# The first norm row of a two-layer decoder trunk: its DMA first in the queue, read from PSUM by the first token tile, the second tile's products behind the first's lo parts

## The chip, the core and the metric

The kernel runs on one core of one Trainium2 chip. The metric is device time in microseconds (us) of one execution. Each version is executed several times; a median of the runs is compared, and one execution is taken by the hardware profiler.

## What is computed

The input `x` has 512 tokens of 1024 features, float32. Two layers follow each other; each is

```python
h = rms_norm(x, pre_mix_norm)
proj = h @ w_in
...
mix = jnp.concatenate([y_ssd, y_sb, y_moba], axis=-1) @ w_out
x = x + rms_norm(mix, post_mix_norm)
h2 = rms_norm(x, pre_ffn_norm)
f = (jax.nn.silu(h2 @ w_gate) * (h2 @ w_up)) @ w_down
return x + rms_norm(f, post_ffn_norm)
```

The mixer in the middle has a state-space part, a stick-breaking attention and a block-sparse attention. For this document only the very first line of the first layer matters: `rms_norm(x, w)` scales each token by one over the root of its mean square and each feature by its gain, `w`, a row of 1024 numbers that is the same for all tokens. The projections behind it are matrix products of the normalised tokens with `w_in`.

## The kernel before, in words

Tokens are cut into four tiles of 128 (`NT`), features into eight of 128 (`KT`). Every float32 product is made of three: an operand is split (`split`, lines 115 to 117) into a hi part, a rounded copy that ScalarE (ACT) writes, and a lo part, the rest, that VectorE (DVE) subtracts. `PASSES` (line 142) multiplies hi by hi, hi by lo and lo by hi, all into one PSUM bank.

The weights come from HBM in chunks of 128 x 1024. `chunk` (line 134) takes a raw buffer from a ring of three, issues its DMA on SyncE's queue (SP) and splits it into a hi and a lo buffer from rings of four.

Before the layers the kernel does this. `load_x` (line 105) loads a token tile as two halves of 512 features. The gain row of the first norm has to stand in all 128 partitions. Each half of it is loaded into one partition (line 125), a matrix product with a column of ones spreads it over a PSUM bank (B6 and B7, line 126), and DVE copies it to SBUF (`grow`, line 127). In lines 249 to 255 the first four weight chunks, which are those of the first projection, are asked for, and every token tile goes through `pre_norm` (line 190). ACT squares and sums each half (line 193); a small add on DVE (line 169) and a power on GpSimd (line 170) make the scale of each token; for each half DVE multiplies tile, scale and row in one instruction (line 196); TensorE transposes the result in eight blocks of 128 x 128 (`to_fm`, line 179) into two banks, B[2t] and B[2t+1] for tile t; and `to_hT` splits each bank into the hi and lo tiles `hT` of the normalised, transposed input.

`tok_proj` (line 211) is the first user of these. For each token tile it runs over the eight feature tiles and the three passes, 24 products of 512 columns into one bank (line 219): B0 for tile 0, B2 for tile 1 and so on, so banks that the transposes of the same tile were written to. Two feature tiles use one weight chunk, so a token tile needs four chunks.

The order on every engine is not that of the source. A planner goes through a simulated time line of the whole program and gives each free engine the ready instruction that stands first in priority: the place in the source, moved ahead by an offset where `tc.high_priority` stands. Splits of chunks are moved ahead by 800 (`SPLIT_OFF`), `pre_norm` of tile 0 by 3000 (`NORM_OFF`). `issue_after`, used by `after` (line 145), adds an edge from one instruction to another on the same engine: the second is placed behind the first.

Of the kernel before, what the change touches and what calls it, by code (L numbers as in the profile page):

```python
# [11 lines left out]
AF = mybir.ActivationFunctionType  # L12
OP = mybir.AluOpType
# [3 lines left out]
P = 128  # L17
D = 1024
S = 512
NT = S // P  # L20
# [38 lines left out]
def trunk(ctx, tc, x, wch, wdt, gains, mixgain, conv, small, ident_d, consts_d, stack_d, out):  # L59
    nc = tc.nc  # L60
    V, A, G, T = nc.vector, nc.scalar, nc.gpsimd, nc.tensor
# [5 lines left out]
    def slot(name, dt=F32, n=512):  # L67
        return cp.tile([P, n], dt, name=name, bufs=1)

    def cut(tiles):  # L70
        return [t[:, h * 512:(h + 1) * 512] for t in tiles for h in range(2)]

    F = [None if 4 <= i < 12 or 18 <= i < 20 or 28 <= i < 40 or i >= 43 else cp.tile([P, 512], F32, name=f"F{i}")
         for i in range(NF)]
    DD = [slot(f"D{i}", F32, D) for i in range(6)]
    RR = [slot(f"RR{i}", F32R, D) for i in range(4)]
    hT = [cp.tile([P, KT, 512], F32R, name=f"hT{a}") for a in range(2)]
    B = [ps.tile([P, 512], F32, name=f"B{i}") for i in range(8)]
# [8 lines left out]
    def sm(n):  # L87
        if used[0] + n > 768:
            used[0] = 0
        used[0] += n  # L90
        return SM[:, used[0] - n:used[0]]

    def ring(items):
        n = [0]

        def take():
            n[0] += 1
            return items[(n[0] - 1) % len(items)]
        return take

    xres = [[slot(f"x{t}{h}") for h in range(2)] for t in range(NT)]
    xsave = dr.tile([NT, P, D], F32, name="xsave")
    ident = cp.tile([P, P], F32, name="ident")

    def load_x(t, src):
        for hf in range(2):
            nc.sync.dma_start(xres[t][hf], src[t][:, hf * 512:(hf + 1) * 512])
# [7 lines left out]
    def split(src, hi, lo, eng=V):  # L115
        A.activation(hi, src, AF.Copy)  # L116
        return eng.tensor_tensor(lo, src, hi.bitcast(F32), op=OP.subtract)  # L117

    load_x(0, x)
    nc.sync.dma_start(ident, ident_d)  # L120
    grow, one = F[20:22], F[24][0:1, 0:P]
    V.memset(one, 1.0)
    for hf in range(2):
        row = F[22 + hf][0:1, :]
        nc.sync.dma_start(row, bass.AP(tensor=gains.tensor, offset=gains[0, 0].offset + hf * 512, ap=[[0, 1], [1, 512]]))
        T.matmul(B[6 + hf], one, row, start=True, stop=True)
        V.tensor_copy(grow[hf], B[6 + hf])
    load_x(1, x)
    mhalf = cp.tile([P, 4], F32, name="mhalf")
    V.memset(mhalf, -0.5)  # L130
# [3 lines left out]
    def chunk(l, i, to=None):  # L134
        raw = take_raw()
        hi, lo = to or (take_hi(), take_lo())
        nc.sync.dma_start(raw, wch[l, i])
        with tc.high_priority(offset=SPLIT_OFF):
            split(raw, hi, lo, G if i in POOL_LO else V)
        return hi, lo  # L140
# [4 lines left out]
    def after(instructions):  # L145
        st = ExitStack()
        for i in instructions:
            st.enter_context(tc.issue_after(i.ins))
        return st
# [14 lines left out]
    def rstd_of(ss_ap, n, rest=None):  # L164
        m, r = sm(n), sm(n)
        if rest is None:
            V.tensor_scalar(m, ss_ap, EPS, None, op0=OP.add)
        else:
            V.tensor_scalar(m, ss_ap, rest, EPS, op0=OP.add, op1=OP.add)
        G.tensor_tensor(r, m, mhalf[:, 0:n], op=OP.pow)  # L170
        return r

    def to_fm(srcs, dst, bank):

        for q in range(0, len(srcs), 4):
            n = min(4, len(srcs) - q)
            p = bank()
            for i in range(n):
                T.transpose(p[:, i * P:(i + 1) * P], srcs[q + i], ident)
            dst(q, n, p)  # L180

    def to_hT(t, keep=None):
        def dst(q, n, p):
            sl = slice(t * P, (t + 1) * P)
            split(p.rearrange("p (k l) -> p k l", k=4), hT[0][:, q:q + n, sl], hT[1][:, q:q + n, sl])
            if keep is not None:
                A.activation(keep[q // 4], p, AF.Copy)
        return dst

    def pre_norm(t, grow, jk, bank, keep=None):  # L190
        ssp = sm(2)
        for hf in range(2):
            A.activation(jk[hf], xres[t][hf], AF.Square, scale=1.0 / 32, accum_out=ssp[:, hf:hf + 1])
        r = rstd_of(ssp[:, 0:1], 1, ssp[:, 1:2])
        for hf in range(2):
            V.scalar_tensor_tensor(jk[hf], xres[t][hf], r[:, 0:1], grow[hf], op0=OP.mult, op1=OP.mult)
        to_fm([jk[i // 4][:, (i % 4) * P:(i % 4 + 1) * P] for i in range(KT)], to_hT(t, keep), bank)

    def post_norm(t, banks, grow, jk, sq, store=None):
# [32 lines left out]
    def fm_proj(l, c, p):  # L232
        w = chunk(l, c)
        fm_mm(p, w, 0, NT, True)
        return p
# [9 lines left out]
    take_jk = ring([F[0:2], F[2:4], F[43:45]])  # L245
# [4 lines left out]
    for t in range(NT):  # L250
        first.append(chunk(0, C_V + t))
        if t > 1:
            load_x(t, x)
        with tc.high_priority(offset=0 if t else NORM_OFF):
            pre_norm(t, grow, take_jk(), ring(B[2 * t:2 * t + 2]))

    cst = cp.tile([P, 2 * P + 512 + 2], F32, name="cst")
    triu = cst[:, 0:P]
# [19 lines left out]
    for l in range(DEPTH):  # L278
# [91 lines left out]
        n = 0  # L370
# [60 lines left out]
        r = rstd_of(ss, 4)  # L431
        for j in range(NT):
            V.scalar_tensor_tensor(MIXA[j][:, 0:256], MIXA[j][:, 0:256], r[:, j:j + 1], MG[1][:, 0:256],
                                   op0=OP.mult, op1=OP.mult)
# [6 lines left out]
        for j in range(NT):  # L441
            w = (j + 1) * P
            sume = sm(4)
            for h in range(4):
# [6 lines left out]
                                       op0=OP.add, op1=OP.min, accum_out=nm[:, 0:1])  # L451
# [7 lines left out]
                for i in range(j + 1):  # L459
                    T.matmul(pv[:, h * 64:(h + 1) * 64], pTs[:, i * P:(i + 1) * P],  # L460
                             VT[i][:, 256 + h * 64:256 + (h + 1) * 64], start=h == 0 and i == 0,
                             stop=h == 3 and i == j, skip_group_check=True)
# [7 lines left out]
            r = rstd_of(ss, 1)  # L470
# [10 lines left out]
        for i in range(8):  # L481
            p = fm_proj(l, C_XBC + i, acc())
            u = XBC[i]
            with tc.high_priority(offset=CONV_OFF):
                A.activation(u, p, AF.Identity, bias=cw[:, i, 4:5], scale=cw[:, i, 3:4])
                for j in range(1, 4):
                    V.scalar_tensor_tensor(u[:, j:], p[:, :S - j], cw[:, i, 3 - j:4 - j], u[:, j:],
                                           op0=OP.mult, op1=OP.add)
# [7 lines left out]
        for c in range(NT):  # L496
            with tc.high_priority(offset=SSD_OFF):
                sl = slice(c * P, (c + 1) * P)
# [27 lines left out]
                for g in range(2):  # L526
# [3 lines left out]
                    for h in range(4):  # L530
                        hh = g * 4 + h
                        T.matmul(py[:, hh * 64:(hh + 1) * 64], L[:, h * P:(h + 1) * P], xdt[:, hh * 64:(hh + 1) * 64],  # L532
                                 start=hh == 0, stop=hh == 7, skip_group_check=True)
                V.tensor_tensor(xd, py, xd, op=OP.add)
                if c > 0:
                    po = mx()
                    for g in range(2):
                        T.matmul(po[:, g * 256:(g + 1) * 256], XBC[6 + g][:, sl], state[:, g * 256:(g + 1) * 256],
                                 start=g == 0, stop=g == 1, skip_group_check=True)
# [17 lines left out]
                r = rstd_of(ss, 2)  # L557
                for g in range(2):
                    gs = slice(g * 256, (g + 1) * 256)
                    V.scalar_tensor_tensor(xd[:, gs], xd[:, gs], r[:, g:g + 1], MG[0][:, gs], op0=OP.mult,  # L560
                                           op1=OP.mult)
# [15 lines left out]
        for pair in range(2):  # L577
            toks = (2 * pair, 2 * pair + 1)
            for q, src in ((1, MIXA), (0, MIX)):
                for j in toks:  # L580
                    p = OB[j][q]
                    with tc.high_priority(offset=MIXT_OFF):
                        for i in range(4):
                            T.transpose(p[:, i * P:(i + 1) * P], src[j][:, i * P:(i + 1) * P], ident)
                        split(p, R[(j % 2) * 4 + q], R[(j % 2) * 4 + 2 + q])
            ks = (4, 5, 6, 7, 0, 1, 2, 3) if pair == 0 else (0, 1, 2, 3, 4, 5, 6, 7)
            for k in ks[0:4]:
                w = w_out[k] if pair else chunk(l, C_OUT + k)
                for j in toks:
                    out_mm(j, k, w, ks)  # L590
            for k in ks[4:8]:
                w_out[k] = chunk(l, C_OUT + k)
            for j in toks:
                for k in ks[4:8]:
                    out_mm(j, k, w_out[k], ks)
                with tc.high_priority(offset=NORM_OFF):
                    post_norm(j, OB[j], grow1, take_jk(), MIXA[j])
                    pre_norm(j, grow2, take_jk(), ring(OB[j] if j < 2 else OB[j][0:1]), QA[j])
# [114 lines left out]
        for t in range(NT):  # L713
            for halves in ((0,), (1,)) if t == NT - 1 else ((0, 1),):
                for i, w, gs in tail:
                    down(i, t, w, gs, halves)
            with tc.high_priority(offset=NORM_OFF):
                post_norm(t, B[2 * t:2 * t + 2], grow3, take_jk(), GT[t], store=out if l + 1 == DEPTH else xsave)
                if l + 1 < DEPTH:
                    pre_norm(t, grow4, take_jk(), ring(B[2 * t:2 * t + 2]))  # L720
# [57 lines left out]
```

## Time and profile before

| | us |
|---|---|
| median of 3 runs | 1231.62 (1230.8, 1231.62, 1232.99) |
| the profiled execution | 1231.86 |
| its span, first to last instruction | 1230.0 |
| mean granted TensorE clock of it | 0.998 |
| TensorE (PE) busy | 1209.0 |
| PE's weight loads busy | 1081.8 |
| DVE busy | 872.0 |
| ACT busy | 604.6 |
| GpSimd (POOL) busy | 52.6 |

A busy time is a sum over the whole span; engines work beside each other. All rows come from the one profiled execution, so they add up to its span and not to the median. In a timeline row an instruction or a run of like instructions stands with its start, the time from there to the end of the last, its engine, its line in the kernel, the tile that it writes and those that it reads, its form, and how many it is. What its engine waited for just before stands in brackets. PEld is the weight load of TensorE, and SPq the DMA queue of SyncE.

### The profile page before, as it was taken

The numbers are of one execution on the slowest core, as the hardware profiler recorded it, in microseconds if no ns is written. First come the engines' busy times: TensorE is split into PE (matmuls) and PEld (weight loads), VectorE is DVE, ScalarE is ACT, GpSimd is POOL, SyncE is SP. The second block draws the span as 40 slices with busy tenths as digits, with TensorE's granted clock in tenths as the row PEclk, the third lists the DMA queues.
The fourth block names the chain that finished last, engine by engine and source line by source line (L and its number), as shares of the span: only waits on it lengthen the run. The fifth ranks groups of instructions, "written<-read, shape, count | busy, mean of one in ns | idle before, by whom it ended". The sixth has DMA issues, their size and how long they took to land.

```text
span 1230.0 us, 19124 instructions
## 1 busy us (share of the span) xinstructions
PE 1209.0 (98%) x7562; PEld 1081.8 (88%) x7562; DVE 872.0 (71%) x1526; ACT 604.6 (49%) x1124; POOL 52.6 (4%) x88
## 2 busy tenths in 40 slices
PE   8999999999999999999999999999999999999997
PEld 6887888889999999888887788888999999998886
DVE  5466856889999998434465577478898899983343
ACT  5556764466444444433445666535654444453231
POOL 1010000010000000000010100001000000000000
PEclk9999999999999999999999999999999999999999
DMA  6332233242333332423423322122523333333321
GB/s 230 120 99 86 76 102 103 70 154 87 104 104 103 107 108 96 130 93 120 137 86 104 133 74 80 67 95 70 171 69 104 104 108 108 110 109 116 99 73 69
DMA packets 40494, 128.42 MB, mean 104 GB/s; under 512 B 5426, under 2 KB 5714, under 8 KB 40404
## 3 DMA queue, kind: packets, MB, share of 16 engines
q1 hardware_dynamic: 39060, 122.97, 30.4%
q0 software_dynamic: 1344, 4.23, 1.0%
q8 instruction: 59, 0.97, 0.3%
q14 instruction: 31, 0.25, 0.1%
HBM read 122.95 MB, written 4.23 MB: 103 GB/s over the span
## 4 chain that ended last, share of the span: by engine, by line
PE 88%; DVE 5%; DMA 2%; ACT 2%; issue 1%; DVEq 0%; POOLq 0%; POOL 0%; ACTq 0%
PE B L631 26%; PE B L698 19%; PE B L228 17%; PE B L219 7%; PE B L572 7%; DMA wr<-in_wch_dram 2%; PE B L347 2%; DVE wl L117 2%; PE B L354 1%; PE B L460 1%; ACT wh L116 1%; PE B L325 1%; PE B L532 1%; PE B L326 1%; PE B L456 1%
## 5 line engine op out<-in xcount | busy, mean ns | idle before, releaser
L117 DVE TENSOR_TENSOR wl<-wr,wh 128x1024 fp32r<-128x1024 f32 (+1 forms) x198 | 219.8, 1113 | 79.7 <-ACT wh L116 78.5
L116 ACT ACTIVATE wh<-wr 128x1024 fp32r<-128x1024 f32 (+1 forms) x198 | 191.3, 968 | 132.2 <-PE B L631 66.1
L228 PE MATMUL B<-hT,wh 128*128 128x512 f32 (+1 forms) x768 | 215.3, 361 | 3.6 <-ACT F L314 2.2
L631 PE MATMUL B<-hT,wh 128*128 128x256 f32 x960 | 193.3, 283 | 0.8 <-ACT F L669 0.7
L631 PE MATMUL B<-D,wh 128*128 128x256 f32 x960 | 185.6, 283 | 0.5 <-ACT wh L116 0.4
L698 PE MATMUL B<-wh,RR 128*128 128x512 f32 x608 | 164.8, 389 | 0.0
L631 PEld LDWEIGHTS B<-hT,wh 128*128 128x128 f32 x960 | 158.1, 192 | 1.6 <-ACT F L669 1.3
L228 PEld LDWEIGHTS B<-hT,wh 128*128 128x128 f32 x768 | 136.0, 190 | 23.4 <-ACT F L314 3.3
L631 PEld LDWEIGHTS B<-D,wh 128*128 128x128 f32 x960 | 154.4, 192 | 1.2 <-ACT wh L116 0.6
L116 ACT ACTIVATE wh<-RR 128x512 fp32r<-128x512 f32 (+1 forms) x120 | 89.2, 770 | 109.1 <-PE B L631 46.5
L228 PE MATMUL B<-hT,wl 128*128 128x512 f32 (+1 forms) x384 | 137.8, 360 | 0.0
L631 PE MATMUL B<-hT,wl 128*128 128x256 f32 x480 | 136.1, 283 | 0.6 <-DVE wl L117 0.4
L631 PE MATMUL B<-D,wl 128*128 128x256 f32 x480 | 135.5, 283 | 0.0
L698 PEld LDWEIGHTS B<-wh,RR 128*128 128x128 f32 x608 | 114.0, 188 | 23.5
L117 DVE TENSOR_TENSOR wl<-RR,wh 128x512 fp32r<-128x512 f32 (+1 forms) x120 | 102.2, 864 | 10.8 <-ACT wh L116 8.7
L117 DVE TENSOR_TENSOR RR<-F,RR 128x512 fp32r<-128x512 f32 x48 | 33.1, 691 | 101.3 <-ACT RR L116 101.3
L698 PE MATMUL B<-wl,RR 128*128 128x512 f32 x304 | 95.4, 389 | 0.0
L631 PEld LDWEIGHTS B<-hT,wl 128*128 128x128 f32 x480 | 92.1, 192 | 1.0 <-DVE wl L117 1.0
L631 PEld LDWEIGHTS B<-D,wl 128*128 128x128 f32 x480 | 92.1, 192 | 0.0
L116 ACT ACTIVATE RR<-F 128x512 fp32r<-128x512 f32 x48 | 30.0, 629 | 122.9 <-PE B L698 122.2
L219 PE MATMUL B<-wh,hT 128*128 128x512 f32 x256 | 82.4, 397 | 0.8 <-DVE hT L117 0.8
L228 PEld LDWEIGHTS B<-hT,wl 128*128 128x128 f32 x384 | 73.1, 190 | 8.9
(210 smaller groups left out, 2005.8 us busy)
## 6 DMA issues: line engine op xcount, KB each, us to landing
wr<-in_wch_dram SPq DMA_DIRECT2D x204, 512.0 KB, 3.6
x<-in_x_dram SPq DMA_DIRECT2D x16, 256.0 KB, 2.9
F<-acd POOLq DMA_DIRECT2D x16, 256.0 KB, 6.4
F<-in_gains_dram SPq DMA_DIRECT2D x14, 256.0 KB, 4.4
xsave<-x SPq DMA_DIRECT2D x8, 256.0 KB, 2.3
x<-xsave SPq DMA_DIRECT2D x8, 256.0 KB, 3.3
out_dram<-x SPq DMA_DIRECT2D x8, 256.0 KB, 2.0
D<-in_mixgain_dram SPq DMA_DIRECT2D x4, 256.0 KB, 4.6
```

The source lines that it names most:

```text
L116: A.activation(hi, src, AF.Copy)
L117: return eng.tensor_tensor(lo, src, hi.bitcast(F32), op=OP.subtract)
L219: T.matmul(p, hT[a][:, k, t * P:(t + 1) * P], w[k // 2][b][:, (k % 2) * 512:(k % 2 + 1) * 512], start=n == 0, stop=n == 3 * KT - 1)
L228: T.matmul(p[:, t0 * P:t1 * P], w[b][:, k * P:(k + 1) * P], hT[a][:, k, t0 * P:t1 * P], start=first and n == 0, stop=n == 3 * KT - 1, skip ...
L325: T.matmul(p, tiles[2 + h][:, cs], tiles[h][:, cd], start=True, stop=False, skip_group_check=True)
L326: T.matmul(p, tiles[2 + h][:, cs], tiles[4 + h][:, cd], start=False, stop=stop, skip_group_check=True)
L347: T.matmul(pz[:, o:w], ntri if i2 == i else nones, s2, start=False, stop=i2 == NT - 1 and n == 1, skip_group_check=True)
L354: T.matmul(pv[:, j * 64:(j + 1) * 64], e[:, (j - i) * P:(j - i + 1) * P], VT[i][:, h * 64:(h + 1) * 64], start=i == NT - 1, stop=i == 0 an ...
L456: T.transpose(pT[:, i * P:(i + 1) * P], lg[:, i * P:(i + 1) * P], ident)
L572: T.matmul(OB[j][hf], lt, w[b][:, hf * 512:(hf + 1) * 512], start=k == ks[0] and a == 0 and b == 0, stop=k == ks[-1] and a == 1)
L631: T.matmul(p, w[b][:, half * 512 + k * P:half * 512 + (k + 1) * P], left(j, a, k), start=first and k == 0 and n == 0, stop=k == 3 and n == ...
L698: T.matmul(B[2 * t + hf], gs[a][:, t * P:(t + 1) * P], w[b][:, hf * 512:(hf + 1) * 512], start=i == 0 and a == 0 and b == 0, stop=i == HT ...
```

## The change

Three things are changed. The two DMAs of the gain row, the two products that spread it, and the copies to `grow` stand ahead of the loads of token tile 0 and the identity; the copies are made by ACT instead of DVE. Token tile 0's products with the row (line 196) read the spread row in PSUM (`spread`, B6 and B7) instead of `grow`; the other tiles still read `grow`. And `done[t]` keeps the last lo instruction of a tile's transposed input; the two products of token tile 1 with the row are placed behind `done[0]`, the lo part of tile 0's second half.

```diff
-    load_x(0, x)
-    nc.sync.dma_start(ident, ident_d)
-    grow, one = F[20:22], F[24][0:1, 0:P]
+    grow, spread, one = F[20:22], B[6:8], F[24][0:1, 0:P]
     V.memset(one, 1.0)
     for hf in range(2):
         row = F[22 + hf][0:1, :]
         nc.sync.dma_start(row, bass.AP(tensor=gains.tensor, offset=gains[0, 0].offset + hf * 512, ap=[[0, 1], [1, 512]]))
-        T.matmul(B[6 + hf], one, row, start=True, stop=True)
-        V.tensor_copy(grow[hf], B[6 + hf])
+        T.matmul(spread[hf], one, row, start=True, stop=True)
+        A.activation(grow[hf], spread[hf], AF.Copy)
+    load_x(0, x)
+    nc.sync.dma_start(ident, ident_d)
     load_x(1, x)
...
+    done = [None] * NT
+
     def to_hT(t, keep=None):
         def dst(q, n, p):
             sl = slice(t * P, (t + 1) * P)
-            split(p.rearrange("p (k l) -> p k l", k=4), hT[0][:, q:q + n, sl], hT[1][:, q:q + n, sl])
+            done[t] = split(p.rearrange("p (k l) -> p k l", k=4), hT[0][:, q:q + n, sl], hT[1][:, q:q + n, sl])
...
-    def pre_norm(t, grow, jk, bank, keep=None):
+    def pre_norm(t, grow, jk, bank, keep=None, hold=()):
...
         for hf in range(2):
-            V.scalar_tensor_tensor(jk[hf], xres[t][hf], r[:, 0:1], grow[hf], op0=OP.mult, op1=OP.mult)
+            with after(hold):
+                V.scalar_tensor_tensor(jk[hf], xres[t][hf], r[:, 0:1], grow[hf], op0=OP.mult, op1=OP.mult)
...
-            pre_norm(t, grow, take_jk(), ring(B[2 * t:2 * t + 2]))
+            pre_norm(t, grow if t else spread, take_jk(), ring(B[2 * t:2 * t + 2]), hold=[done[0]] if t == 1 else ())
```

## Rows read from the trace of the kernel before

**Rows 1.** The page, part 1: busy us (share of the span) and instructions of each engine.

```profile
PE 1209.0 (98%) x7562; PEld 1081.8 (88%) x7562; DVE 872.0 (71%) x1526; ACT 604.6 (49%) x1124; POOL 52.6 (4%) x88
```

**Rows 2.** Waits of PE, whole span: us in total, times, longest; largest behind the start.

```profile
PE B L228 <- ACT F L314: 2.2, 4, 0.7
```

**Rows 3.** Timeline of PE, 0 to 24 us.

```profile
4.28 3.75 PE L126 MATMUL B<-F,F 1*128 1x512 f32 x4 [4.28 <-DMA F<-in_gains_dram]
7.96 1.12 PE L179 MATMUL B<-ident,F 128*128 128x128 f32 x4
9.55 2.82 PE L179 MATMUL B<-ident,F 128*128 128x128 f32 x12 [0.48 <-DVE F L196]
12.61 0.79 PE L219 MATMUL B<-wh,hT 128*128 128x512 f32 x1 [0.24 <-DVE hT L117]
13.21 0.63 PE L219 MATMUL B<-wl,hT 128*128 128x512 f32 x1
13.63 0.70 PE L219 MATMUL B<-wh,hT 128*128 128x512 f32 x2
...
```

**Rows 4.** The chain that ended last, in order of time: start us, us, what.

```profile
12.61 9.02 PE B L219 x36
...
23.38 13.62 PE B L219 x60
...
99.97 4.61 PE B L228 x19
...
705.51 6.22 PE B L228 x19
```

**Rows 5.** Timeline of DVE, 0 to 24 us.

```profile
5.27 0.23 DVE L273 CAST identb<-ident 128x128 bf16<-128x128 f32 x1 [4.28 <-DMA ident<-in_ident_dram]
5.41 0.21 DVE L169 TENSOR_SCALAR SM<-SM 128x1 f32<-128x1 f32 x1
6.35 0.69 DVE L127 COPY F<-B 128x512 f32<-128x512 f32 x1 [0.73 <-PE B L126]
7.15 0.75 DVE L196 SCALAR_TENSOR_TENSOR F<-x,SM,F 128x512 f32<-128x512 f32 x1
...
8.06 0.69 DVE L127 COPY F<-B 128x512 f32<-128x512 f32 x1
8.74 2.08 DVE L196 SCALAR_TENSOR_TENSOR F<-x,SM,F 128x512 f32<-128x512 f32 x3
10.74 1.22 DVE L117 TENSOR_TENSOR wl<-wr,wh 128x1024 fp32r<-128x1024 f32 x1
11.88 0.68 DVE L117 TENSOR_TENSOR hT<-B,hT 128x512 fp32r<-128x512 f32 x1
...
20.50 1.22 DVE L117 TENSOR_TENSOR wl<-wr,wh 128x1024 fp32r<-128x1024 f32 x1
```

**Rows 6.** Timeline of SP's DMA queue, 0 to 24 us.

```profile
0.74 0.87 SPq L107 DMA_DIRECT2D x<-in_x_dram  x2
...
2.12 0.61 SPq L125 DMA_DIRECT2D F<-in_gains_dram  x2
```

**Rows 7.** Timeline of ACT, 0 to 24 us.

```profile
3.52 0.63 ACT L193 ACTIVATE F<-x 128x512 f32<-128x512 f32 x1 [1.50 <-DMA x<-in_x_dram]
...
8.47 1.06 ACT L116 ACTIVATE wh<-wr 128x1024 fp32r<-128x1024 f32 x1 [0.64 <-DMA wr<-in_wch_dram]
9.44 0.58 ACT L116 ACTIVATE hT<-B 128x512 fp32r<-128x512 f32 x1
...
19.06 1.06 ACT L116 ACTIVATE wh<-wr 128x1024 fp32r<-128x1024 f32 x1 [1.24 <-DMA wr<-in_wch_dram]
```

**Rows 8.** Timeline of POOL, 0 to 24 us.

```profile
5.77 0.55 POOL L170 TENSOR_TENSOR SM<-SM,mhalf 128x1 f32<-128x1 f32 x1 [2.80 <-DVE SM L169]
```

**Rows 9.** Waits of SP's DMA queue, 0 to 40 us: us in total, times, longest.

```profile
SPq L137 <- DMA cst<-in_consts_dram: 0.7, 1, 0.7
```

**Rows 10.** One stretch: PE, PEld, DVE, ACT, POOL busy, PEclk, DMA share, GB/s.

```profile
708.00:710.00 2.00, 2.00 (x6) 1.52 (x6) 1.08 (x2) 0.27 (x1) 0.00 (x0) 0.50 0.00 0
```

## The prediction

> **What bounds the kernel now.** I read the page first. TensorE (PE) is busy for 1209.0 of 1230.0 us [rows 1], so a change that touches no matmul of the layers can only move what stands before the first of them, or a wait of PE further on. The list of PE's waits says how little there is of the second kind: behind the start the largest group is 2.2 us in four waits [rows 2]. So I read the first 24 us engine by engine. PE's timeline [rows 3] shows the four broadcast matmuls of the norm row at 4.28, the transposes of the first token tile at 7.96, a run of twelve more from 9.55 (four of tile 0, eight of tile 1), and the first projection product at 12.61. From there the chain of waits is PE alone: 36 products to 21.63, then transposes, then 60 products from 23.38 in 13.62 us, 0.227 each [rows 4]. Whatever brings the product of 12.61 forward, and only that, moves the end.
>
> What holds it is VectorE (DVE) [rows 5]. The first product writes the bank that the transposes of tile 0 went to, so it waits for the lo part that reads that bank: 11.88 + 0.68 = 12.56. In front of it in DVE's order stand a copy of the spread row (6.35), the first product with the row (7.15, "tile product" from here, line 196), a second copy (8.06), three tile products from 8.74 (one of tile 0, two of tile 1), and the lo part of the first weight chunk (10.74).
>
> **The change, step by step.**
>
> *The row's DMAs go first.* Two issues of 0.61 us together now begin at 2.12 [rows 6]; they move to the head of the queue, where the first x load began at 0.74, 1.38 us earlier. The broadcasts follow with the distance they have now: from 4.28 to about 2.9, four in 3.75 us, so the first half is spread by 4.95 (now 6.35, when the copy starts) and the second by 6.65 (now 4.28 + 3.75 = 8.03) [rows 3, 5].
>
> *What it passes on SP:* the two loads of x tile 0 and the identity, each 0.61 later. x tile 1 and the weight chunks keep their place behind the same five issues, so the first chunk still lands at 8.47, where ScalarE (ACT) waits for it [rows 7]. ACT's squares of tile 0 move from 3.52 to 4.13. On DVE the identity's cast (5.27) stands ahead of the tile's small add (5.41); the power on GpSimd takes until 5.77 + 0.55 = 6.32 [rows 8]. All 0.61 later, the scale is ready at 6.93.
>
> *The tile products of tile 0 read PSUM.* The first starts at 6.95 instead of 7.15, the second 0.7 behind it, at 7.65 instead of 8.74. If the planner lets the add pass the cast, they start 0.4 earlier still. That a product reads PSUM I cost at nothing: DVE's PSUM copy takes 0.69, its product from SBUF 0.75 [rows 5]; from those rows its bounds are minus 0.06 and plus 0.69 for two. Work hides it too, for tile 0 is ready about 1 us before the weights are (next step).
>
> *The copies move to ACT.* DVE loses 2 x 0.69 = 1.4 us, ACT gains two of about 0.58, the time of its PSUM read at 9.44 [rows 7]. ACT is waiting for x or for the chunk in most of the time before 8.47, so I cost them at nothing. Without that cover, with both in front of the chunk's hi part, they cost 1.2 us. They read banks that tile 3's transposes use again, and those come behind 21.63 [rows 4].
>
> *The hold.* DVE's two tile products of tile 1 (the last two of the run of three at 8.74, 2/3 of its 2.08, 1.4 us) wait for the last lo part of tile 0. They have no semaphore to wait for, since the lo part is on the same engine; the order alone changes. Behind them are tile 1's eight transposes on PE, its hi and lo parts, and its products.
>
> *Sum at the first product.* The chunk now decides: hi part 8.47 + 1.06 = 9.53, tile 0's hi part to 10.02 [rows 7], then on DVE the chunk's lo part to 10.77 and tile 0's lo part to 11.45. The first product comes at 11.45, 1.16 earlier. If DVE takes tile 0's lo part first, the first product comes at 10.75, but the second, which needs the chunk's lo part, at 11.9 against 13.21, 1.3 earlier [rows 3]. Both orders agree within 0.15 us.
>
> *What 1.16 us is worth.* The first products are slow: start to start 0.42 (13.21 to 13.63) against 0.227 later [rows 3, 4]. 512 columns in 0.42 is the lower level, 1.2 GHz; the engine goes over to 2.4 GHz at about 13.65, after the transposes and one us of products. If the rise comes at the same time as now, the 1.16 us are filled with 2.75 slow products, worth 2.75 x 0.227 = **0.6 us**; the other order's 1.3 give 0.7; I take 0.65. If the rise comes forward with the products, all 1.16 stays. If it comes later, the gain is lost (a rival below).
>
> The Trainium skill, "TensorE: Matmul & The Clock Gate", Part 1, says that the throttled state is the default and that sustained activity releases it. That speaks against this change: tile 1's transposes, which keep PE busy from 9.55 to the first product, are moved behind it, and by the rule the rise would come later and the sum be a loss of about 1 us.
>
> *What is late next.* Tile 1: on DVE, from 11.45, the second lo part of tile 0 (0.65), a chunk's lo part (1.2), the two tile products (1.4), another chunk (1.2) and the first lo part of tile 1 (0.65) end at 16.55. PE wants it after tile 0's 18 products, now at 21.4 - 18 x 0.227 = 17.3, then at 16.65: just covered. If DVE is later by half a us, most of the gain is gone, so the low end of the gain is 0. Then the fourth chunk: its DMA is held in SP's queue until an earlier load has landed [rows 9], ACT waits for it until 19.06 [rows 7] and its lo part ends at 20.50 + 1.22 = 21.72. None of this moves. The products that need it start at 23.38, so the gain cannot exceed 1.66 us.
>
> **Sum:** 1231.86 (the profiled execution: span 1230.0 and 1.9 around it) - 0.65 = 1231.2. That execution lies 0.24 above the median of 1231.62, so the forecast for a median is **1231.0**, with 0 to 1.66 us of gain: 1230.0 to 1231.6.
>
> **The rivals.**
>
> *A: TensorE stays at the lower level longer* (slower). PE stands idle from the end of tile 0's transposes, about 9.7, to 11.45. What a stretch at the lower level costs is shown further on: in layer 1 the granted clock is 0.50 of full from 708 to 710, the lower level [rows 10], and the 19 products from 705.51 take 6.22 us, while the same 19 of layer 0, from 99.97, take 4.61 [rows 4]: 1.6 us. One more such stretch at the start gives 1231.0 + 1.6 = 1232.6, 1.0 slower than before. It decides from the point where the rise comes over 0.65 / 0.46 = 1.4 us later than 13.65 (each us at the lower level loses 1 - 0.227 / 0.42 = 0.46). For it: PE's busy stretch before the rise is cut in two. Against it: the broadcasts and tile 0's transposes stay, and more products stand before 13.65.
>
> *B: the fall in layer 1 goes, or layer 0 gets one.* Both layers have the same work and waits there and only one fell, so a small shift can turn it. One fewer: 1231.0 - 1.6 = 1229.4, and with the largest gain 1228.4. One more: 1232.6.
>
> *C: the planner orders later work otherwise.* The order of each engine is laid out over the whole program. It can take away the 2.2 us of [rows 2] or add as much: 1228.8 to 1233.2, or 1 beyond on either side where the start goes its bad or best way. Against it: PE is the bound from 12.61 on, and an order laid out around it should shift as a whole.
>
> *D: it does nothing.* DVE orders the lo parts of tile 0 behind other work as now, and tile 1 eats what tile 0 gained: 1231.6.
>
> **How the numbers follow.** A measurement of this kernel can tell about 0.2% from no change, 2.5 us. Chances: forecast 0.47; A 0.15; B 0.13 for one fall fewer and 0.09 for one more; C 0.10, D 0.06. Faster by over 2.5 us needs one fall fewer with over 0.85 us of gain at the start (0.07) or the good side of C (0.04): 0.11. Slower by over 2.5 needs A and one more fall together (0.03) or the bad side of C (0.04): 0.07. Same: 0.82. Range: from 1229.0, which leaves out the faster tail, to 1233.0, above A and B, which leaves out the bad side of C.
>
> **What would show it.** After: the row's DMAs at 0.74, the broadcasts near 2.9; no copy on DVE, two on ACT before 8.47; DVE's tile products of tile 0 near 7 and 7.7, those of tile 1 behind tile 0's second lo part; the first product near 11.45, a start-to-start of 0.42 until about 13.65, and the 60 products from about 22.7. The forecast is wrong if the first product comes no earlier than 12.3, if the products are still slow beyond 15, or if the 60 products move by 0.65 and the end doesn't.

## The result, and the profile after

The changed kernel takes 1241.06 us (median of four runs, 1239.09 to 1242.22), the kernel before 1232.11 (four runs, 1230.8 to 1232.99): a ratio of **1.0068** (1.0055 to 1.008). It is slower by 8.4 us by the ratio and 9 by the medians, far above the range. The profiled execution took 1239.09 us with a span of 1237.3, 7.3 more than the span before, at a granted clock of 0.998, the same as before. The page's part 1 says first where the 7.3 us are not [rows 1]:

```profile
PE 1210.5 (98%) x7562; PEld 1082.3 (87%) x7562; DVE 871.8 (70%) x1524; ACT 605.5 (49%) x1126; POOL 53.1 (4%) x88
```

PE does the same 7562 instructions in 1.5 us more; the other 5.8 us it stands idle. DVE lost two instructions and ACT gained two, as the diff says.

**The start.** PE's timeline of the changed kernel, in the columns of [rows 3]:

```profile
2.20 3.75 PE L124 MATMUL B<-F,F 1*128 1x512 f32 x4 [2.20 <-DMA F<-in_gains_dram]
7.57 1.97 PE L179 MATMUL B<-ident,F 128*128 128x128 f32 x8 [1.62 <-DVE F L199]
13.17 0.79 PE L222 MATMUL B<-wh,hT 128*128 128x512 f32 x1 [3.63 <-DVE hT L117]
13.76 0.63 PE L222 MATMUL B<-wl,hT 128*128 128x512 f32 x1
14.19 1.05 PE L222 MATMUL B<-wh,hT 128*128 128x512 f32 x2
...
16.75 0.79 PE L222 MATMUL B<-wh,hT 128*128 128x512 f32 x2
...
18.08 1.04 PE L179 MATMUL B<-ident,F 128*128 128x128 f32 x8
18.87 0.47 PE L222 MATMUL B<-wl,hT 128*128 128x512 f32 x1
```

The broadcasts come 2.1 us earlier. The transposes of tile 0 are done at 9.54, then PE waits 3.63 us, and the first product comes at 13.17, 0.56 later than before [rows 3]. Start to start the products are still 0.43 apart until 16.75 (before: until 13.63). Tile 1's eight transposes, which filled the wait before the first product, now stand among the products at 18.08. DVE's timeline shows what the first product waits for [rows 5]:

```profile
6.77 1.45 DVE L199 SCALAR_TENSOR_TENSOR F<-x,SM,B 128x512 f32<-128x512 f32 x2 [0.74 <-POOL SM L170]
...
11.29 1.23 DVE L117 TENSOR_TENSOR wl<-wr,wh 128x1024 fp32r<-128x1024 f32 x1 [1.43 <-ACT wh L116]
12.43 0.68 DVE L117 TENSOR_TENSOR hT<-B,hT 128x512 fp32r<-128x512 f32 x1
...
14.77 1.41 DVE L199 SCALAR_TENSOR_TENSOR F<-x,SM,F 128x512 f32<-128x512 f32 x2
```

Tile 0's two products with the row start at 6.77, read PSUM and take 0.72 each; tile 1's stand behind tile 0's lo parts at 14.77. All that is as the change wants it. But DVE then waits for ACT's hi part of the first weight chunk, and ACT's timeline says why [rows 7]:

```profile
4.60 0.58 ACT L125 ACTIVATE F<-B 128x512 f32<-128x512 f32 x1
...
6.86 0.58 ACT L125 ACTIVATE F<-B 128x512 f32<-128x512 f32 x1
8.89 0.63 ACT L195 ACTIVATE F<-x 128x512 f32<-128x512 f32 x1 [1.45 <-DMA x<-in_x_dram]
...
10.20 1.06 ACT L116 ACTIVATE wh<-wr 128x1024 fp32r<-128x1024 f32 x1 [0.59 <-DMA wr<-in_wch_dram]
```

The two copies of the spread row fit into waits. ACT takes up the second half of token tile 1, as it lands, at 8.89 and the first chunk at 10.20. In the trace before it squared the one at 7.11 and rounded the other at 8.47 [rows 7]:

```profile
7.11 0.63 ACT L193 ACTIVATE F<-x 128x512 f32<-128x512 f32 x1 [0.26 <-DMA x<-in_x_dram]
```

Yet SP issues them when it did. The timeline of its queue in the changed kernel:

```profile
0.74 0.64 SPq L123 DMA_DIRECT2D F<-in_gains_dram  x2
...
2.77 0.91 SPq L107 DMA_DIRECT2D x<-in_x_dram  x2
3.72 1.38 SPq L137 DMA_DIRECT2D wr<-in_wch_dram  x3
```

and in the kernel before:

```profile
2.77 0.83 SPq L107 DMA_DIRECT2D x<-in_x_dram  x2
3.65 1.38 SPq L137 DMA_DIRECT2D wr<-in_wch_dram  x3
```

The transfers, not the issues, are late: in the three us from 5 to 8 the DMA engines move 198, 217 and 258 GB/s, before 309, 307 and 356.

**The middle of layer 1.** The start explains 2.8 us: the first product of the feature-major projection (line 231, 228 before) starts at 39.6 instead of 36.8, first before, then after:

```profile
36.83 0.62 PE L228 MATMUL B<-hT,wh 128*128 128x512 f32 x2
39.62 0.62 PE L231 MATMUL B<-hT,wh 128*128 128x512 f32 x2
```

Followed from stage to stage by the first start of their lines on PE, layer 0 adds -0.3, layer 1's mixer +3.4, its output projection +2.2, and the feed-forward part gives back 0.8: with the start 7.3. The list of PE's waits from 640 us on begins with one that the kernel before doesn't have (its longest single wait there is 0.9):

```profile
PE B L525 <- DVE D L518: 2.1, 1, 2.1
PE B L231 <- ACT F L317: 1.1, 2, 0.7
```

PE's timeline at that place in the kernel before, where the line is 522, in the state-space part of the mixer:

```profile
793.67 0.27 PE L508 MATMUL B<-ident,F 128*128 128x128 f32 x1
793.70 0.48 PE L219 MATMUL B<-wh,hT 128*128 128x512 f32 x1
...
799.41 0.61 PE L456 MATMUL B<-ident,D 128*128 128x128 f32 x4
799.85 0.61 PE L522 MATMUL B<-F,F 128*128 128x128 f32 x4
```

Between the last of four transposes (line 508) and line 522, 6 us of other work, most of it products, cover what DVE does with the bank. In the changed kernel the same instructions stand thus:

```profile
795.75 0.33 PE L511 MATMUL B<-ident,F 128*128 128x128 f32 x1 [0.19 <-ACT F L162]
796.27 0.33 PE L511 MATMUL B<-ident,F 128*128 128x128 f32 x1 [0.19 <-ACT F L162]
798.66 1.11 PE L525 MATMUL B<-F,F 128*128 128x128 f32 x4 [2.07 <-DVE D L518]
799.43 0.77 PE L222 MATMUL B<-wh,hT 128*128 128x512 f32 x1
800.00 0.63 PE L222 MATMUL B<-wl,hT 128*128 128x512 f32 x1
800.43 1.05 PE L222 MATMUL B<-wh,hT 128*128 128x512 f32 x2
```

Nothing stands between, the products that covered the wait come right behind it, and they are 0.43 us apart: 512 columns in that time is 1.2 GHz, the lower of the clock's two levels. Windows of the changed kernel (PE, PEld, DVE, ACT, POOL busy, PEclk, which is the granted clock as a share of the full one, DMA share, GB/s):

```profile
13.00:15.00 2.00, 1.83 (x4) 1.49 (x5) 2.00 (x4) 2.00 (x5) 0.00 (x0) 1.00 1.05 408
...
104.00:108.00 4.00, 4.00 (x23) 3.42 (x22) 2.14 (x3) 1.45 (x3) 0.00 (x0) 1.00 0.23 89
...
796.00:800.00 4.00, 1.74 (x7) 1.41 (x7) 2.07 (x4) 3.74 (x8) 0.00 (x0) 0.84 0.13 46
800.00:804.00 4.00, 4.00 (x15) 3.19 (x14) 1.53 (x3) 0.00 (x0) 0.00 (x0) 0.73 0.00 0
...
830.00:840.00 10.00, 8.19 (x50) 6.34 (x48) 8.73 (x17) 1.89 (x6) 0.70 (x1) 1.00 0.01 2
```

and of the kernel before at the like places:

```profile
794.00:798.00 4.00, 4.00 (x19) 3.30 (x18) 2.48 (x4) 1.42 (x3) 0.00 (x0) 1.00 0.00 0
798.00:802.00 4.00, 4.00 (x28) 3.60 (x27) 1.47 (x3) 0.72 (x2) 0.00 (x0) 1.00 0.00 0
...
824.00:834.00 10.00, 9.11 (x57) 7.71 (x56) 9.71 (x20) 1.50 (x5) 1.07 (x1) 1.00 0.01 2
```

PE is idle for 2.26 us of the window from 796, the granted clock is 0.73 in the next, and the output projection is idle for 0.9 us more at 830 (1.81 against 0.89). (The first two windows are for the last section.) What is the same in the two programs is as telling: PE's instructions stand in the same order in all of layer 0 behind the start and in everything behind layer 1's output projection. Only the start and one stretch of layer 1 differ, from 712 to 892 us in the trace before: 1039 of PE's records, and at 696 of these places another instruction stands. No line of the diff touches that stretch; the planner laid it out otherwise.

### The profile page after: what moved, and what is told of

Same layout as the page of the kernel before. It is cut to its first block, busy times and chain, and to the rows that moved or that the text cites. A ratio compares the mean times of both kernels' runs of the same rounds, so it can differ in the third digit from the quotient of the medians.

```text
span 1237.3 us, 19124 instructions
## 1 busy us (share of the span) xinstructions
PE 1210.5 (98%) x7562; PEld 1082.3 (87%) x7562; DVE 871.8 (70%) x1524; ACT 605.5 (49%) x1126; POOL 53.1 (4%) x88
## 4 chain that ended last, share of the span: by engine, by line
PE 93%; DVE 3%; ACT 2%; issue 1%; DMA 1%; SPq 0%; DVEq 0%; POOLq 0%; POOL 0%; ACTq 0%
PE B L634 32%; PE B L701 19%; PE B L231 17%; PE B L222 7%; PE B L575 6%; PE B L350 2%; PE B L357 1%; PE B L463 1%; PE B L535 1%; PE B L328 1%; PE B L329 1%; DMA wr<-in_wch_dram 1%; PE B L179 1%; PE B L459 1%; ACT wh L116 1%
```

## The experiments

By now three theories stood: that the time goes at the start (row first, or the hold), that it goes in layer 1's other order, or that ACT's copies and the PSUM read cost something. All ratios are to the kernel before on the same chip.

**e1, the change without the hold.**

```diff
-            pre_norm(t, ..., hold=[done[0]] if t == 1 else ())
+            pre_norm(t, ..., hold=())
```

> The change without the hold on tile 1's products with the row; the row's DMAs first, the PSUM read and the ACT copies stay. Theory 1 (the hold is the cause, in two places: it puts tile 1's transposes and a longer time at the lower TensorE level on the start, and it turns the planner's order of layer 1's mixer): first weight chunk still lands late (near 10.2), first product near 13.1, lower level only until about 14, first line-231 product near 37.3 (before 36.8, changed 39.6), layer 1 from its first line-231 product to its first line-575 product in about 165 to 166.5 us as before (changed 169.7), total 0 to 1 us above before. Rival 2 (the row's DMAs at the head cost the start, the later chunk): first line-231 product near 39 to 39.6 and total 2 to 3 above before. Rival 3 (the late start itself turns layer 1, not the hold): total about 5 above before.

Measured: 1.0016 (1.0007 to 1.0026), 2.0 us, above theory 1's 0 to 1. Layer 1 has the order of before, as theory 1 has it, but the start is rival 2's: the first line-231 product comes at 39.3. The very first product comes at 13.72, for chunk and tile land as late as with the change: ACT's square of tile 1's second half starts at 8.88, the chunk's hi part at 10.09. PE's timeline, with tile 1's transposes in front of the first product again:

```profile
11.32 1.97 PE L179 MATMUL B<-ident,F 128*128 128x128 f32 x8 [1.77 <-DVE F L199]
13.72 0.79 PE L222 MATMUL B<-wh,hT 128*128 128x512 f32 x1 [0.43 <-DVE hT L117]
```

Without the hold 2.0 us of the loss are left, so the hold carries most of it, in one way or another.

**e2, the hold alone.**

```diff
+            with after(hold):
-                V.scalar_tensor_tensor(jk[hf], ...)
+                    V.scalar_tensor_tensor(jk[hf], ...)
```

(with `done` as in the change; the head and `grow` as before)

> Before with the hold alone; DMA order, DVE copies and the SBUF row as before. Theory 1: first chunk lands at 8.5 as before, first product near 11.5, the lower TensorE level lasts until 13.7 to 16.8, first line-231 product at 37 to 38.5, layer 1's mixer over 3 us longer than before, total 4 to 7 above before. Rival 2 (the row's DMAs): total within 1 of before. Rival 3 (late start turns layer 1): with a start no more than 1.5 later, layer 1 as before, total 0 to 1.5 above.

Measured: 1.0087 (1.0072 to 1.0103), 10.7 us, above the 4 to 7 of theory 1. Layer 1's order is that of the change but for 229 of PE's records, all from 805 us on, and its output projection takes 93.0 us, nearly as there (93.3; before 91.1). The hold alone brings the whole loss. ACT takes up the first chunk at 9.18, and PE's first product comes 0.46 earlier than before:

```profile
9.18 1.06 ACT L116 ACTIVATE wh<-wr 128x1024 fp32r<-128x1024 f32 x1 [1.80 <-DMA wr<-in_wch_dram]
12.15 0.79 PE L222 MATMUL B<-wh,hT 128*128 128x512 f32 x1 [1.51 <-DVE hT L117]
```

Even so the first line-231 product comes at 39.5, 2.7 later than before: the hold delays the start without a late first product.

**e3, the row first alone.**

```diff
-    load_x(0, x)
-    nc.sync.dma_start(ident, ident_d)
     grow, one = F[20:22], F[24][0:1, 0:P]
...
         V.tensor_copy(grow[hf], B[6 + hf])
+    load_x(0, x)
+    nc.sync.dma_start(ident, ident_d)
```

> Before with the row's DMAs, products and DVE copies ahead of the loads of x tile 0 and the identity, nothing else. Theory 1: first chunk lands late, at about 10 instead of 8.5, and first product 0.5 to 1 later than 12.6; layer 1 as before; total 0 to 1.5 above before. Rival 2: total 2 to 3 above before. If the chunk lands at 8.5, the late landing was no matter of the DMA order but of that execution.

Measured: 1.0014 (1.0003 to 1.0026), as e1, with the late landings of e1 (9.00 and 10.23). So the row first, by itself, costs 1.7 us (0.4 to 3.2), a little more than the 0 to 1.5 expected.

**e4, PSUM read and ACT's copies alone.**

```diff
+    load_x(0, x)
+    nc.sync.dma_start(ident, ident_d)
     for hf in range(2):
...
+            pre_norm(t, ..., hold=())
```

(against the change; the two lines behind the loop are gone)

> Before with the PSUM read of tile 0 and the copies on ACT, no hold, DMA order as before. Theory 1: first chunk at 8.5, DVE 1.4 us less busy before the first product, first product near 12.0, layer 1 as before, total 0 to 1 below before. Rival (the ACT copies stand ahead of something late): first product at 12.6 or later, total at or above before.

Measured: 0.9999 (0.9989 to 1.0009). Within 1.4 us these two parts cost nothing and give nothing. The first product didn't come near 12.0. In this execution the chunk was late though the loads stand as before:

```profile
9.88 1.06 ACT L116 ACTIVATE wh<-wr 128x1024 fp32r<-128x1024 f32 x1 [1.31 <-DMA wr<-in_wch_dram]
12.85 0.80 PE L222 MATMUL B<-wh,hT 128*128 128x512 f32 x1 [0.62 <-DVE hT L117]
```

**e5 and e6, the kernel before with one or two more copies on DVE.** They write a row that is there already; what they do is to delay DVE at the start by 0.69 us each. Neither has a hold or anything else of the change.

```diff
+    for _ in range(1):        # e6: range(2)
+        V.tensor_copy(grow[1][:, 0:512], B[7][:, 0:512])
     load_x(1, x)
```

> Before with one more DVE copy of the second half of the spread row (0.69 us, the same values written again); no part of the change. Built, its order in layer 1's mixer (positions 3872 to 4681 of TensorE's 6958 rows) is that of the changed kernel, layer 0's is that of before. Theory 1 (what the change costs is mainly the planner's other order of layer 1's mixer): layer 1 from its first line-231 or 228 product to the end 4 to 7 longer than before's, start 0.5 to 1 later, total 5 to 8 above before. Rival (the changed start is the cost): total 0.5 to 1 above before.

> As the kernel with one copy, with two copies (1.4 us); its order in layer 1 is that of before again. Theory 1: start 1 to 1.5 later, layer 1 as before, total 1 to 1.5 above before, so 4 to 6 less than with one copy. Rival: total above that of one copy.

Measured: **1.0093** (1.0076 to 1.011) with one copy and 1.0037 (1.0024 to 1.005) with two. One copy of 0.69 us costs 11.5 us, and two cost less than one, 4.6. Both are above what was expected (5 to 8, and 1 to 1.5); that two cost less was expected. PE's waits behind 640 us of e5:

```profile
PE B L524 <- DVE D L517: 2.1, 1, 2.1
```

and the longest group of e6's:

```profile
PE B L230 <- ACT F L316: 1.1, 2, 0.7
```

With one copy layer 1's mixer has the order of the changed kernel, with its wait; with two it has that of before. The order doesn't need the hold: one copy's delay turns it. In both kernels tile 1's eight transposes stand behind the first products, as with the hold; e6 keeps before's order all the same, so that alone doesn't turn it. The 6.9 us between e5 and e6 are the order's price, less what the second copy adds.

**e7 and e11, the change with three or two such copies.** If the order makes the loss, the whole change, hold and all, should lose much less where the copies happen to restore it.

```diff
+    for _ in range(3):        # e11: range(2)
+        V.tensor_copy(grow[1][:, 0:512], B[7][:, 0:512])
     load_x(1, x)
```

> The changed kernel with all its parts and three more DVE copies (2.1 us) of the spread row's second half; its order in layer 1 is that of before. Theory 1: start as in the changed kernel or up to 1 later, layer 1 as before, total 1.5 to 4 above before and 4 to 7 below the changed kernel. Rival (the start with the hold is the cost): total 8 to 11 above before.

> The changed kernel with two more DVE copies of the row's second half. As built, layer 1 has the order of before and layer 0's mixer (rows 395 to 2916) one that neither kernel has. Theory 1 (an order of the mixer has its price, whichever layer it is in): layer 1 as before, layer 0 from its first line-231 product to its first line-575 product another time than 164.7 to 166.3, to either side by 1 to 5; total by as much from that with three copies, 1236.0. Rival (the hold or the start is the cost): total as the changed kernel's.

Measured: e7 1.0037 (1.0024 to 1.005) with before's order in layer 1; e11 1.0085 (1.0072 to 1.0098). In e11 layer 1 has before's order too, and now layer 0 has the other one. Its PE waits between 30 and 640 us begin with

```profile
PE B L527 <- DVE D L520: 2.1, 1, 2.1
```

and layer 0's mixer takes 171.4 us against 166.3 (a layer with one clock fall), its output projection 93.3 against 91.1. Its order there is that of e2's layer 1 but for 64 places. So the other order costs 5.1 and 2.2 us in layer 0 as well, less 0.5 in the feed-forward part. By the total alone the rival would fit too; the stages decide. In e7 the loss is 4.6 us, a little above the 1.5 to 4 expected and far below the rival's 8.

**e8, the hold on the second half only.** Tile 1's first half isn't held, the second is, and layer 1 may come out otherwise.

```diff
-            with after(hold):
+            with after(hold if hf else ()):
```

> The changed kernel with the hold on the second half of tile 1 alone; its order in layer 1 is that of before. Theory 1: layer 1 as before, total 1 to 3 above before (the row's DMAs first cost about 2, four transposes less move into the products). Rival (the hold at the start is the cost): about half of the change's 8, 4 or more.

Measured: 1.0032 (1.002 to 1.0044), with before's order in layer 1. So e7 and e8 show the change, or most of it, without the other order: 3.9 to 4.6 us slower than before. For e8 1 to 3 was expected, so it lies at the edge of the rival, by which the start costs 4 or more. Less the 2.0 of e1, 2.0 to 2.6 us would be the hold's own (e7's includes what its copies cost); the intervals leave it between about 0.5 and 4. That the two parts add up isn't shown: e2 and e6, with the row where it was, lose as much as the change and e7.

**e9 and e10, no hold and the loads in other order.** Both keep the row early; e9 takes its DMAs off SP's queue, e10 moves the identity behind token tile 1.

```diff
-        nc.sync.dma_start(row, ...)
+        nc.scalar.dma_start(row, ...)
```

```diff
-    nc.sync.dma_start(ident, ident_d)
     load_x(1, x)
+    nc.sync.dma_start(ident, ident_d)
```

> The change without the hold, the row's two DMAs issued from ACT's queue, so that x tile 0 and the identity keep their places at the head of SP's; order of layer 1 as before. Theory 1 (the row's place ahead of x on SP is what makes the first chunk land late and costs some 2 us): ACT's squares start near 3.5, the first chunk lands at 8.4 to 9.9 as in the runs with x first, first product near 12.2, total within 1 of before. Rival (the row's two DMAs ahead of x slow the transfers whatever queue they leave from): chunk at 10 or later, total 1.5 to 2.5 above before. ACT has one more table load in this build, 1.3 us between its first two squares, which either theory covers by the wait for the chunk.

> The change without the hold, row first on SP, the identity's load moved behind x tile 1's; order of layer 1 as before. If the identity's short packets among the x loads cause the slow transfers between 4.8 and 7.5 us, the second half of x tile 1 comes before 7.5 (8.9 in the changed kernel) and the first chunk at about 9; if it is the row ahead of x, both stay at 8.9 and 10.1. Total: 0 to 1 above before in the first case, 1.5 to 2.5 in the second.

Measured: 1.0006 (0.9996 to 1.0016) and 1.0006 (0.9995 to 1.0017): the landings come part of the way back, and nothing is gained. Both ratios lie below e1's, but the intervals overlap, so that a part of the 2 us comes back with the landings isn't shown. ACT's timeline of e10:

```profile
7.29 0.63 ACT L195 ACTIVATE F<-x 128x512 f32<-128x512 f32 x1 [0.17 <-DMA x<-in_x_dram]
...
9.32 1.06 ACT L116 ACTIVATE wh<-wr 128x1024 fp32r<-128x1024 f32 x1 [1.30 <-DMA wr<-in_wch_dram]
```

In e10 tile 1 is there nearly as early as before, the chunk 0.9 earlier than in the change and 0.85 later than in the trace before; in e9 ACT takes them up at 8.19 and 9.43. Why the transfers are late with two small loads ahead and the issues in place stays open.

**e12, the changed kernel once more**, for the spread between executions.

> The changed kernel once more, for its time beside before on one chip and a second profile of its start. Theory 1: 8 to 10 above before, layer 1 longer by 4 to 6 than before's, the first chunk at about 10, the first product near 13. If the start differs by over 1 us from the first profile, what the first profile shows of the clock's rise is one execution's.

Measured: 1.0079 (1.0063 to 1.0095), profiled at 1243.61. The wait, the clock's fall and the output projection (93.3) are there again:

```profile
104.00:108.00 4.00, 4.00 (x12) 3.14 (x12) 2.14 (x3) 1.94 (x5) 0.00 (x0) 0.57 0.29 116
...
798.00:802.00 4.00, 2.07 (x13) 1.29 (x12) 1.33 (x3) 3.99 (x9) 0.00 (x0) 1.00 0.19 66
802.00:806.00 4.00, 3.29 (x12) 2.77 (x13) 2.28 (x4) 1.78 (x4) 0.00 (x0) 0.74 0.00 0
```

From layer 1's first feature-major product to the last down product it takes 587.8 us, e7, which has the other order and the same falls, 580.8: the 7 us once more. By the times of whole runs the same comparison (the two sets of the change against e7) gives 3.8 and 5.2 by ratios, 5.1 and 6.6 by medians.

## Why the prediction was wrong

It was wrong: 1231.0 with a range to 1233.0, and 1241 came. The loss has two parts: layer 1's order, 4 to 7 us, and the start, where the change without that order (e7, e8) loses 3.9 to 4.6. The row first costs 1.7 to 2 of the start when there is no hold; what it adds beside the hold isn't shown. By the steps of the prediction:

- **The step that failed most** is in rival C: "an order laid out around it should shift as a whole", with a bound of 2.2 us. The order didn't shift: at 696 of 1039 places of layer 1, 712 us and more into the run, another instruction stands. The bound was drawn from waits that stand in the trace before [rows 2]. But a new order can uncover work that products covered and that shows as no wait at all: the 2.07 us of DVE's work in front of line 525 was covered before. From the trace, the price is 2.07 of wait, 0.6 in three waits for ACT before it, 1.4 for the seven products at the lower level from 799.43 to 802.39 (2.96 us instead of 7 x 0.227) and 0.4 for line 525 itself at that level: 4.4 of the 5.0 that the mixer lost if the old fall at 706 [rows 10], which this execution didn't have, is taken out of the time before (169.7 against 166.3 less 1.6). The output projection adds 2.2, of which 0.9 is idle time at 830; the rest wasn't followed. What in the planner's simulated line turns the order stays open; a copy of 0.7 us on DVE does it, two of them don't (e5, e6).
- **"The first chunk still lands at 8.47"** failed: it landed at 10.20. Put into the prediction's own sum, 11.45 + (10.20 - 8.47) = 13.18, and the first product came at 13.17. The chain through the chunk's hi part, its lo part and tile 0's lo part was right, one term of it wrong by 1.7 us: the 2.97 us from the chunk to the first product stand in e2, e4 and e12 too. But 8.47 was one execution's figure. With the loads in before's order ACT takes up the chunk at 8.38 to 9.88 (before, e2, e4, e5, e6), with the row first on SP's queue and the identity ahead of tile 1 at 9.49 to 10.73 (the change, e1, e3, e7, e8, e11, e12), so a part of the 1.7 us can be chance. The second half of tile 1 keeps these groups apart, 6.66 to 7.11 against 7.89 to 9.51. Without a hold, the late landing goes with the 1.7 to 2 us of e1 and e3.
- **The hold, "the order alone changes"**, was costed at nothing. It moves tile 1's eight transposes from a time when PE had nothing else into the stream of products: 0.8 us (18.08 to 18.87). And with the late chunk it leaves PE idle for 3.63 us before the first product (1.51 in e2, where the chunk is earlier). The forecast took the rise "at the same time as now", 13.65; it came behind 16.75. So rival A had the direction: 3.58 us of products at the lower level instead of 1.02, and at its own rate 2.56 x 0.46 = 1.2 us. With 0.56 for the first product and 0.8 for the transposes that makes 2.6 of the 2.8 us at line 231. The premise that only the product of 12.61 moves the end failed with it: e2 has its first product at 12.15 and line 231 2.7 us later than before, e10 has 13.06 and line 231 0.1 earlier, at 36.7. What differs is the time at the lower level, 5.7 us in e2 and 0.3 in e10.
- That the lower level lasts longer behind the hold shows in more than one execution. In the six traces with all of tile 1's transposes in front of the first product (before, e1, e3, e4, e9, e10) the products run at that level for 0.3 to 4.0 us, mean 2.0. In the five with the full hold (the change, e2, e7, e11, e12) it is 3.6 to 5.7, mean 5.2. The other three, where the copies or half a hold put transposes behind it (e5, e6, e8), have 3.2 to 5.3. The means are far apart, but the ranges overlap: e1 has 4.0 without a hold, the change 3.6 with one. The Trainium skill, "TensorE: Matmul & The Clock Gate", Part 1, has the lower level as the default that sustained activity releases, and by that rule the rise had to come later; the traces agree in the mean.
- **Right:** that the broadcasts and the first product with the row come early (2.20, forecast 2.9; 6.77, forecast 6.95, with the add behind the cast as before), PSUM read at SBUF's price (0.72 against 0.75), ACT's copies in the waits, tile 1 behind tile 0 on DVE. All of it is worth nothing (e4), since the chunk decides.
- The signs that the prediction set for being wrong came: a first product after 12.3 and products at the lower level beyond 15.

No version beat the kernel before.

## What to carry to other kernels

Where an order is planned over the whole program, a small edit is two experiments in one: its own effect, and a new order somewhere else, which here cost more than any part of the edit. Compare the instruction order of the two programs before reading times, and try the edit with a meaningless delay or two beside it: if a delay of 0.7 us alone moves the time by 11 us, the edit hasn't been measured yet. And a wait that fills an engine with work of later tiles isn't idle time to be cut: what stood in it has to be done somewhere.

## What the runs showed of the hardware

**A clock fall that comes and goes.** Rival B was drawn from one fall in layer 1 and none in layer 0. Both occur in some executions and not in others, with the same program: the window 104 to 108 has a granted clock of 1.00 in the first trace of the change and 0.57 in e12, shown above, after the same 1.64 us of idle time of PE between 100 and 104. With before's order a mixer takes 164.7 us without such a fall and 166.2 to 166.4 with it. Part of the spread between executions (1230.1 to 1235.0 us in 25 runs of the kernel before) is no matter of the program. The fall behind the uncovered wait is another matter: it stands in all five traces with the other order, at 798 to 804 us in layer 1 (the change, e2, e5, e12) and at 197 us in layer 0 (e11), and in no trace without that order.

**The start's lower level varies as much.** The kernel before and e4 give PE nearly the same work to the first product (12.61 and 12.85), and their products run at the lower level for 1.02 and 3.58 us. The changed kernel, one and the same program, has 3.58 us in its first trace and 5.71 in e12. "TensorE: Matmul & The Clock Gate" of the Trainium skill, Part 1, calls the number of products at the lower level "run-variable" for one kernel, which these traces bear out. The granted clock doesn't show this first stretch: it reads 1.00 for 13 to 15 us in the change's windows, while products are 0.43 us apart. Its level has to be read from the distance between products.
